# Pairs of 512-column subtractions joined into 1024-column ones, one more convolution job in seven products, and ScalarE's output work emitted later

## The chip, the cores and the metric

The kernel runs on one core of a Trainium2 chip. The metric is the device time of one execution in microseconds (us), the median of several runs. A profiled execution of the same program gives the trace.

The engines are called as in the profile: PE (TensorE matmuls), PEld (its weight loads, which overlap PE), DVE (VectorE), ACT (ScalarE), POOL (GpSimd) and SP (which only issues DMAs here).

## The reference

One layer of a hybrid decoder on x of 512 positions by 1024 channels, in float32:

```
h = rmsnorm(x, norm_mix_g)
proj = h @ w_in                       # 1024 x 9232
bg, cg, xv, q, k, v, z, a, b, ga, gb = split(proj)
y_a = (bg * causal_dwconv(cg * xv, conv_a_w)) @ w_a_out
y_b = gdn_branch(q, k, v, z, a, b, ...) @ w_b_out
mix = sigmoid(ga) * y_a + sigmoid(gb) * y_b
x = x + mix @ w_o
h = rmsnorm(x, norm_ffn_g)
up = causal_dwconv(h @ w_up, ffn_conv_w);  gate, val = split(up)
x = x + (silu(gate) * val) @ w_down
return rmsnorm(x, norm_final_g)
```

`gdn_branch` is a gated delta rule over 8 heads of 128, in chunks: a recurrence of small matmuls. bg, cg, xv, ga, gb, q, k, v and z have 1024 columns each; w_up has 5632.

## The kernel before

**Jobs.** The products with weights are cut into jobs of 256 output columns, and `run_jobs` (L225) runs them one after the other. The order is: 16 jobs for k, q, v and z of the delta rule; GB0 to GB3; then the convolution jobs CG0, XV0, BG0, CG1, XV1, BG1 and so on to BG3; GA0 to GA3; then w_a_out, w_b_out, w_o, w_up and w_down. While PE works on job i, the weights of job i+1 are prepared and those of job i+2 to i+4 are loaded, 1 MB a job in four quarters of 128x512.

**Precision.** Every operand is split into a rounded high part and the rest: ACT casts a 128x512 quarter to the high part `wh` (L159), and DVE subtracts it from the quarter for the low part `wl` (L160). `mm3` (L117) then makes three matmuls for each product (high x low, low x high, high x high). `wh` and `wl` are pools of WQ = 12 tiles each; a new tile waits until PE has read the tile that was there.

**Plain jobs.** `col_job` (L261) makes 2 output banks x 8 row tiles x 3 = 48 matmuls of 512 columns, from four quarters.

**Seven-product jobs.** `sum_job` (L320) cuts the 1024x256 weight block and the activations into 2x2 quarters and makes seven products in place of eight (a Strassen form): 7 x 4 x 3 = 84 matmuls of 256 columns. For this `SumBlock.split` (L174) prepares seven forms, called 11, 12, 22, s3, s2, s4 and s1, of which the last four are sums of quarters: four DVE operations on the raw block (L182), seven casts and seven subtractions. PE uses the forms in the order 11, 12, s3, s2, s4, 22, s1 in three banks A, B, C. Four `snap` copies on ACT (L139) save a bank's half while PE goes on: u after 11, v after s3, u after s2, v after s4. Form s2 writes over what the first u copy reads, 22 over what the first v copy reads, s1 over what the second u copy reads; so PE waits for these copies.

**Outputs.** After 22 `firsts` (L346) is queued, after s1 `seconds` (L350): each is one DVE addition (L347, L351) that makes half of the job's output, and `seconds` goes on with the job's consumer: a sigmoid on ACT for GB and GA; for XV a multiplication by CG's output (L1262) and a convolution of one ACT operation (L391) and two DVE taps (L394) for each half; for BG two multiplications (L1271); nothing for CG.

**What sets the order.** PE, ACT and DVE each run their queue strictly in the program's order. The kernel's Python writes the order: after each 2048 columns of matmuls `tick` (L96) takes a step of each of several queues of generators: one of the delta rule's three (backs, mids, chains), two of `evacs` (the outputs), one of `splits` (the next block's preparation), one of `sums_of`. A `yield` ends a step. A scheduler then orders the instructions that are ready, and `tc.issue_after` (L135) keeps the s casts and the consumers behind the last snap.

Of the 28 jobs that could go in seven products, 27 do: GB1 to GB3, all convolution jobs but XV1 (L1279), GA0 to GA2, and ten of w_up. XV1 is plain.

Of the kernel before, what the change touches and what calls it, by code (L numbers as in the profile page):

```python
# [9 lines left out]
F32 = mybir.dt.float32  # L10
F32R = mybir.dt.float32r
AF = mybir.ActivationFunctionType
ALU = mybir.AluOpType
# [3 lines left out]
P = 128  # L17
S = 512
# [8 lines left out]
C_BG, C_CG, C_XV, C_Q, C_K, C_V, C_Z, C_GA, C_GB = range(0, 36, 4)  # L27
# [4 lines left out]
WQ = 12  # L32
# [29 lines left out]
def layer_kernel(ctx, tc, x, norm_mix_g, w_in, w_ab, conv_a_w, gdn_conv_w, gdn_A_log, gdn_dt_bias,  # L62
# [3 lines left out]
    pe, act, dve, pool = nc.tensor, nc.scalar, nc.vector, nc.gpsimd  # L66
# [6 lines left out]
    wp = ctx.enter_context(tc.tile_pool(name="wp", bufs=2))  # L73
# [3 lines left out]
    def nm(s):  # L77
        cnt[0] += 1
        return f"{s}{cnt[0]}"

    def bank():
        return ps.tile([P, 512], F32, tag="ps", name=nm("ps"))
# [50 lines left out]
    snaps = []  # L133

    def after(ins):  # L135
        return tc.issue_after(ins) if ins else nullcontext()

    def snap(out, in_):
        snaps.append(act.copy(out=out, in_=in_).ins)  # L139

    class Block:
        def __init__(self, src, quarter=(4, P)):
            self.src, self.quarter = src, quarter
            self.raw, self.ready, self.lead, self.fed, self.fine = None, False, 2, True, False
            self.wh, self.wl, self.behind = {}, {}, None
# [6 lines left out]
            for lo, hi in [(q, q + 1) for q in range(4)] if self.fine else [(0, 4)]:  # L152
                nc.sync.dma_start(out=self.raw[:, lo:hi], in_=src[:, lo:hi])

        def part(self, name, src):
            wh = wp.tile([P, S], F32R, tag="wh", bufs=WQ, name=nm("wh"))
            wl = wp.tile([P, S], F32R, tag="wl", bufs=WQ, name=nm("wl"))
            with after(snaps[-1] if name in ("s1", "s2", "s3", "s4") and snaps else self.behind):
                act.copy(out=wh, in_=src)  # L159
            dve.tensor_tensor(out=wl, in0=src, in1=wh.bitcast(F32), op=ALU.subtract)  # L160
            self.wh[name], self.wl[name] = (t if len(self.quarter) == 1 else t.rearrange("p (k n) -> p k n", n=P)
                                            for t in (wh, wl))

        def split(self):
            if self.ready:
                return
            self.ready = True
            for q in range(4):
                self.part(q, self.raw[:, q])
                yield  # L170


# [1 line left out]
    class SumBlock(Block):  # L174
        def split(self):
            if self.ready:
                return
            self.ready = True
            r = [self.raw[:, q] for q in range(4)]

            def to(q, a, b, op):
                dve.tensor_tensor(out=r[q], in0=a, in1=b, op=op)  # L182

            self.part("11", r[0])
            yield
            self.part("12", r[1])
            yield
            self.part("22", r[2])
            yield
            to(2, r[3], r[2], ALU.add)  # L190
            to(3, r[0], r[3], ALU.subtract)
            self.part("s3", r[3])
            yield
            to(0, r[2], r[0], ALU.subtract)
            self.part("s2", r[0])
            yield
            to(1, r[1], r[0], ALU.subtract)
            self.part("s4", r[1])
            yield
            self.part("s1", r[2])  # L200
            yield


    class FormBlock(Block):
# [12 lines left out]
        def split(self):  # L217
            if self.ready:
                return
            self.ready = True  # L220
            for q, name in enumerate(self.names):
                self.part(name, self.raw[:, q])
                yield

    def run_jobs(jobs):  # L225
# [35 lines left out]
    def col_job(w, i, xs, consume, pre=None):  # L261
        def use(wh, wl):
            if pre:
                pre()
            x_ = xs() if callable(xs) else xs
            for j in range(GW // P):
                o = bank()
                products(o, wh, wl, j, x_)
                evacs.append(Task(consume(j, o)))
        return Block(lambda: w[i]), use  # L270
# [49 lines left out]
    def sum_job(w, i, xs, sums, consume, place, pre=None, uv=None, near=lambda: None):  # L320
        def use(wh, wl):
            if pre:
                pre()
            drain(sums_of)
            x_, ts, low = xs() if callable(xs) else xs, sums(), near()
            A, B, C = bank(), bank(), bank()
            L, R = slice(0, HS), slice(HS, S)
            dst = place()
            u, v = uv() if uv else (scratch("u"), scratch("v"))

            def times(o, form, b, first):
                mm3(o, [(wh[form][:, k], wl[form][:, k], b[0][:, k], b[1][:, k]) for k in range(ND // 2)],
                    first, not first)

            def quarter(K, T):
                if K and low:
                    return [low[e][T] for e in range(2)]
                return [x_[e][:, K * 4:K * 4 + 4, T * HS:T * HS + HS] for e in range(2)]

            def t(i_):  # L340
                return [ts[e][i_] for e in range(2)]

            d = dst.rearrange("p (j t c) -> p t j c", j=2, t=2)
            pair = lambda a: a.rearrange("p (j c) -> p j c", j=2)

            def firsts():  # L346
                dve.tensor_tensor(out=d[:, 0], in0=pair(B), in1=pair(u), op=ALU.add)  # L347
                yield

            def seconds():  # L350
                dve.tensor_tensor(out=d[:, 1], in0=A[:, L].unsqueeze(1).broadcast_to([P, 2, HS]), in1=pair(v),  # L351
                                  op=ALU.add)
                yield
                yield
                for j in range(2):
                    rest = consume(j, dst[:, j * S:(j + 1) * S])
                    while True:
                        with after(snaps[-1]):
                            got = next(rest, rest)
                        if got is rest:  # L360
                            break
                        yield

            times(A[:, L], "11", quarter(0, 0), True)
            snap(u[:, L], A[:, L])
            times(B[:, L], "12", quarter(1, 0), True)
            times(B[:, R], "s3", t(2), False)
            snap(v[:, R], B[:, R])
            times(A[:, L], "s2", t(1), False)
            snap(u[:, R], A[:, L])  # L370
            times(C[:, L], "s4", quarter(1, 1), True)
            snap(v[:, L], C[:, L])
            times(B[:, R], "22", t(3), False)
            evacs.append(Task(firsts()))
            times(A[:, L], "s1", t(0), False)
            evacs.append(Task(seconds()))
        return SumBlock(lambda: w[i]), use

# [39 lines left out]
    hT = [hp.tile([P, ND, S], F32R, tag=f"h{i}", name=f"hT{i}") for i in range(2)]  # L418
# [100 lines left out]
    with tc.tile_pool(name="st1", bufs=1) as st1:  # L519
# [80 lines left out]
        def out_lo(lo, bs, k):  # L600
            dve.scalar_tensor_tensor(out=hT[1][:, k, lo:lo + HS], in0=bs[k // 2][:, (k % 2) * HS:(k % 2 + 1) * HS],  # L601
                                     scalar=wA[:, 120 + k:121 + k], in1=hT[0][:, k, lo:lo + HS].bitcast(F32),
                                     op0=ALU.mult, op1=ALU.subtract)

        def round_k(q):
            wh = wp.tile([P, S], F32R, tag="wh", bufs=WQ, name=nm("wh"))
            act.copy(out=wh, in_=k_block.raw[:, q])
            k_block.wh[q] = wh.rearrange("p (k n) -> p k n", n=P)

        def rest_k(q):  # L610
            wl = wp.tile([P, S], F32R, tag="wl", bufs=WQ, name=nm("wl"))
            dve.tensor_tensor(out=wl, in0=k_block.raw[:, q], in1=k_block.wh[q].rearrange("p k n -> p (k n)").bitcast(F32),
                              op=ALU.subtract)
            k_block.wl[q] = wl.rearrange("p (k n) -> p k n", n=P)
# [552 lines left out]
    hsums = lambda: st["ts"]  # L1167
# [90 lines left out]
    def xv_c(g):  # L1258
        def c(j, o):
            m = 2 * g + j  # L1260
            u = held[g][:, j * S:(j + 1) * S]
            dve.tensor_tensor(out=u, in0=o, in1=u, op=ALU.mult)  # L1262
            c_ = tmp("c", 2)
            yield from conv(c_, u, ca_w(m), 3)
            held["c", m] = c_
        return c
# [8 lines left out]
    near = lambda: st.get("near")  # L1275
    for g in range(4):
        jobs += [sum_job(w_in, C_CG + g, hT, hsums, nothing, cg_place(g), None if g else open_conv,
                         near=near if g else lambda: None),
                 sum_job(w_in, C_XV + g, hT, hsums, xv_c(g), pair_out, near=near) if g != 1 else  # L1279
                 col_job(w_in, C_XV + g, hT, xv_c(g)),  # L1280
                 sum_job(w_in, C_BG + g, hT, hsums, bg_c(g), pair_out, near=near)]

    def ga_c(g):
# [343 lines left out]
    def xs():  # L1627
        if "xs" not in st:
            st["xs"] = [place(st["up"], f"t{e}", f"xs{e}") for e in range(2)]
        return st["xs"]  # L1630
# [208 lines left out]
```

## Time and profile before

| what | before |
|---|---|
| median of 3 runs | 945.96 us (945.27 to 946.88) |
| the profiled execution | 946.38 us |
| its span | 944.6 us |
| PE busy | 932.1 us (99%) |
| PEld busy | 823.0 us (87%) |
| DVE busy | 777.0 us (82%) |
| ACT busy | 546.4 us (58%) |
| granted PE clock | 1.00 nearly throughout |

The span runs from the first to the last instruction; 1.8 us of the execution lie outside it. A timeline row has the start in us, the duration, the engine, the line, the operation, out<-in, the shapes and a count; in square brackets stands the idle time of the engine before it and what ended it. A row with a count is several instructions in a run. A matmul's duration is longer than its distance to the next one, since they are pipelined, so PE's pace is read from starts. DVE's and ACT's instructions overlap at their ends too.

### The profile page before, as it was taken

The page shows a single profiled execution, that of the slowest core. Times are in us where ns is not written, and L with a number is a line of the kernel's source. Part 1 is how long each engine was busy: PE and PEld are TensorE (multiplying, and loading weights), DVE is VectorE, ACT ScalarE, POOL GpSimd, SP SyncE. Part 2 cuts the span into 40 slices and gives each one's busy share as a digit, 9 for nine tenths or more (in the row PEclk, how much of TensorE's full clock was granted, in tenths as well). Part 3 has the DMA queues.
Part 4 walks back from the last instruction along what each step waited for, and adds up shares of the span by engine and source line. Part 5 has one row for each costly group of instructions (what it writes and reads, how often), then busy time and mean ns, then how long its engine had stood idle before and what let it go on. Part 6 is the DMA issues. An engine that isn't in the chain of part 4 may idle for free.

```text
span 944.6 us, 17664 instructions
## 1 busy us (share of the span) xinstructions
PE 932.1 (99%) x6512; PEld 823.0 (87%) x6512; DVE 777.0 (82%) x1448; ACT 546.4 (58%) x1202; POOL 177.5 (19%) x288
## 2 busy tenths in 40 slices
PE   8999999999999999999999999999999999999996
PEld 6888887887889999999988888998899998888885
DVE  5978686898967989999753579998899898988885
ACT  6796756666465554555741246455565566556563
POOL 3330401304111121312342000322322210000001
PEclk9999999999999999999999999999999999999998
DMA  6443422213014568776797336586966675187332
GB/s 232 158 141 99 121 55 91 76 48 105 9 47 135 154 199 170 174 196 182 246 256 175 111 131 217 154 215 178 226 156 221 153 187 139 48 286 245 106 100 89
DMA packets 82902, 142.41 MB, mean 151 GB/s; under 512 B 24795, under 2 KB 29824, under 8 KB 80256
## 3 DMA queue, kind: packets, MB, share of 16 engines
q1 hardware_dynamic: 65904, 107.47, 34.7%
q0 software_dynamic: 16768, 33.56, 17.9%
q8 instruction: 51, 0.84, 0.3%
q14 instruction: 35, 0.29, 0.1%
q10 hardware_dynamic: 144, 0.26, 0.1%
HBM read 133.64 MB, written 32.78 MB: 176 GB/s over the span
## 4 chain that ended last, share of the span: by engine, by line
PE 85%; DVE 6%; ACT 3%; issue 2%; DMA 2%; POOL 1%; SPq 0%; POOLq 0%; DVEq 0%; ACTq 0%
PE ps L109 78%; DVE raw L182 2%; DVE wl L160 2%; PE ps L819 1%; PE ps L784 1%; DMA xt<-in_x_dram 1%; ACT wh L159 1%; PE ps L1022 1%; PE ps L1042 1%; DVE c L394 1%; PE ps L1031 1%; DMA raw<-in_w_in_dram 0%; PE ps L1010 0%; PE ps L1009 0%; PE ps L1480 0%
## 5 line engine op out<-in xcount | busy, mean ns | idle before, releaser
L159 ACT CAST wh<-raw 128x512 fp32r<-128x512 f32 x377 | 218.4, 621 | 129.2 <-PE ps L109 77.5
L160 DVE TENSOR_TENSOR wl<-raw,wh 128x512 fp32r<-128x512 f32 x377 | 251.0, 688 | 40.8 <-ACT wh L159 38.8
L109 PE MATMUL ps<-hT,wh 128*128 128x512 f32 (+1 forms) x888 | 251.6, 360 | 0.3 <-DVE hT L601 0.3
L109 PEld LDWEIGHTS ps<-hT,wh 128*128 128x128 f32 x888 | 156.9, 189 | 20.7 <-DVE hT L601 0.5
L109 PE MATMUL ps<-hT,wl 128*128 128x512 f32 (+1 forms) x444 | 152.1, 353 | 0.0
L109 PE MATMUL ps<-h,wh 128*128 128x512 f32 (+1 forms) x592 | 150.2, 341 | 0.0
L109 PEld LDWEIGHTS ps<-h,wh 128*128 128x128 f32 x592 | 103.2, 189 | 12.5
L109 PE MATMUL ps<-ts,wh 128*128 128x256 f32 x544 | 100.7, 279 | 1.6 <-ACT u L139 1.6
L109 PE MATMUL ps<-wh,xs 128*128 128x512 f32 (+1 forms) x320 | 96.5, 384 | 0.0
L109 PE MATMUL ps<-h,wl 128*128 128x512 f32 (+1 forms) x296 | 96.0, 340 | 0.0
L109 PEld LDWEIGHTS ps<-hT,wl 128*128 128x128 f32 x444 | 83.8, 189 | 9.8
L109 PEld LDWEIGHTS ps<-ts,wh 128*128 128x128 f32 x544 | 84.9, 188 | 2.3 <-ACT u L139 2.2
L182 DVE TENSOR_TENSOR raw<-raw 128x512 f32<-128x512 f32 x108 | 74.3, 688 | 2.6
L109 PEld LDWEIGHTS ps<-wh,xs 128*128 128x128 f32 x320 | 59.6, 188 | 11.8
L109 PE MATMUL ps<-ts,wl 128*128 128x256 f32 x272 | 65.5, 277 | 0.0
L249 POOL COPY gate<-raw 1x1 f32<-1x1 f32 x38 | 22.1, 581 | 215.7 <-DMA raw<-in_w_up_dram 77.6
L109 PEld LDWEIGHTS ps<-h,wl 128*128 128x128 f32 x296 | 56.0, 189 | 6.3
L109 PE MATMUL ps<-wl,xs 128*128 128x512 f32 (+1 forms) x160 | 61.4, 384 | 0.0
L109 PE MATMUL ps<-us,wh 128*128 128x256 f32 x320 | 57.9, 277 | 0.0
L394 DVE SCALAR_TENSOR_TENSOR ct<-ps,wA,ct 128x511 f32<-128x511 f32 (+2 forms) x72 | 53.2, 741 | 3.9 <-ACT ct L391 3.7
L159 ACT CAST wh<-raws 128x512 fp32r<-128x512 f32 x66 | 39.7, 620 | 25.6 <-DVE wl L160 8.1
L160 DVE TENSOR_TENSOR wl<-raws,wh 128x512 fp32r<-128x512 f32 x66 | 43.3, 687 | 11.5 <-ACT wh L159 11.5
(341 smaller groups left out, 1792.2 us busy)
## 6 DMA issues: line engine op xcount, KB each, us to landing
raw<-in_w_up_dram SPq DMA_DIRECT2D x88, 256.0 KB, 4.6
raw<-in_w_in_dram SPq DMA_DIRECT2D x20, 1024.0 KB, 5.2
raw<-in_w_in_dram SPq DMA_DIRECT2D x64, 256.0 KB, 4.4
dv<-in_w_down_dram POOLq DMA_DIRECT2D x50, 256.0 KB, 6.8
raws<-in_w_down_dram SPq DMA_DIRECT2D x32, 256.0 KB, 4.4
raws<-dv SPq DMA_DIRECT2D x24, 256.0 KB, 5.3
ov<-in_w_o_dram POOLq DMA_DIRECT2D x20, 256.0 KB, 6.3
raw<-in_w_a_out_dram SPq DMA_DIRECT2D x16, 256.0 KB, 5.0
```

What stands on the lines that cost most here:

```text
L109: pe.matmul(o, lhsT=a, rhs=b, start=start, stop=stop, skip_group_check=free)
L159: act.copy(out=wh, in_=src)
L160: dve.tensor_tensor(out=wl, in0=src, in1=wh.bitcast(F32), op=ALU.subtract)
L182: dve.tensor_tensor(out=r[q], in0=a, in1=b, op=op)
L249: tc.keep_in_program_order(pool.tensor_copy(out=gate[:, 0:1], in_=el[:, 0:1]))
L394: dve.scalar_tensor_tensor(out=dst[:, sh:], in0=src[:, :S - sh], scalar=wcol(j), in1=dst[:, sh:], op0=ALU.mult, op1=ALU.add)
L784: pe.transpose(out=o[:, n * P:(n + 1) * P], in_=src[:, n * P:(n + 1) * P], identity=ident)
L819: pe.matmul(o[:, i], lhsT=kqs[:, a, h, 0, sl], rhs=kqs[:, b, h, :, sl], start=a > 0, stop=a + b == 0)
L1022: pe.matmul(o[:, 0:P], lhsT=TTf[:, f, :], rhs=rs[h], start=True, stop=True)
L1031: pe.matmul(o2[:, 0:P], lhsT=kn[:, f, :], rhs=vns[h], start=True, stop=True)
L1042: pe.matmul(o[:, 0:P], lhsT=A[:, f, :], rhs=vns[h], start=True, stop=True)
```

## The change

1. The two pools of 12 tiles become two tiles of 12 slots each (`ringh`, `ringl`), given out in turn. `parts` casts one or two quarters and makes one subtraction over both where their slots are neighbours: 1024 columns; a pair that falls on slots 11 and 0 is still two of 512.
2. In `SumBlock.split` the forms go in pairs: (11, 12), then 22 alone, (s3, s2), (s4, s1). The four sums are the same four numbers, made in another order: s3 is now the first sum made, where it was the second.
3. In `seconds` the consumer begins four yields, not two, behind the addition.
4. XV1 becomes a `sum_job`.

```diff
+    ring = [wp.tile([P, WQ, S], F32R, bufs=1, name=n) for n in ("ringh", "ringl")]
...
-        def part(self, name, src):
-            wh = wp.tile([P, S], F32R, tag="wh", bufs=WQ, name=nm("wh"))
-            wl = wp.tile([P, S], F32R, tag="wl", bufs=WQ, name=nm("wl"))
-            with after(snaps[-1] if name in ("s1", "s2", "s3", "s4") and snaps else self.behind):
-                act.copy(out=wh, in_=src)
-            dve.tensor_tensor(out=wl, in0=src, in1=wh.bitcast(F32), op=ALU.subtract)
...
+        def parts(self, names, qs):
+            at = ring_slots(len(names))
+            for name, q, a in zip(names, qs, at):
+                with after(snaps[-1] if name in ("s1", "s2", "s3", "s4") and snaps else self.behind):
+                    act.copy(out=ring[0][:, a], in_=self.raw[:, q])
...
+            cut = next((i for i in range(1, len(at)) if at[i] < at[i - 1]), len(at))
+            for lo, hi in ((0, cut), (cut, len(at))):
+                if lo < hi:
+                    wh, wl = (t[:, at[lo]:at[hi - 1] + 1] for t in ring)
+                    step = qs[1] - qs[0] if len(qs) > 1 else 1
+                    dve.tensor_tensor(out=wl, in0=self.raw[:, qs[lo]:qs[hi - 1] + 1:step], in1=wh.bitcast(F32),
+                                      op=ALU.subtract)
...
-            self.part("11", r[0])
-            yield
-            self.part("12", r[1])
-            yield
-            self.part("22", r[2])
-            yield
-            to(2, r[3], r[2], ALU.add)
-            to(3, r[0], r[3], ALU.subtract)
-            self.part("s3", r[3])
-            yield
-            to(0, r[2], r[0], ALU.subtract)
-            self.part("s2", r[0])
-            yield
-            to(1, r[1], r[0], ALU.subtract)
-            self.part("s4", r[1])
-            yield
-            self.part("s1", r[2])
+            self.parts(("11", "12"), (0, 1))
+            yield
+            yield
+            self.parts(("22",), (2,))
+            yield
+            to(0, r[0], r[3], ALU.subtract)
+            to(3, r[3], r[2], ALU.add)
+            yield
+            to(2, r[2], r[0], ALU.subtract)
+            self.parts(("s3", "s2"), (0, 2))
+            yield
+            to(1, r[1], r[2], ALU.subtract)
+            yield
+            self.parts(("s4", "s1"), (1, 3))
             yield
...
-                yield
-                yield
+                for _ in range(4):
+                    yield
...
-                 sum_job(w_in, C_XV + g, hT, hsums, xv_c(g), pair_out, near=near) if g != 1 else
-                 col_job(w_in, C_XV + g, hT, xv_c(g)),
+                 sum_job(w_in, C_XV + g, hT, hsums, xv_c(g), pair_out, near=near),
```

What it moves in the engines' queues is shown at three places. The line numbers of the changed kernel are higher by up to 14: L160 becomes L175, L182 L196, L347 L358, L351 L362, L159 L167, L1061 L1075, L1285 L1298.

ACT's queue at the start of job GA1, before. `mixa` is the output of the job in front, GA0, and L1285 its sigmoid, which waits for GA0's `seconds`; u and v are GA1's snaps; the casts belong to the next block.

```order
L159 CAST wh_5927<-raw_67 128x512 [waits DMAHW5_49,Activation_49]
L159 CAST wh_5941<-raw_67 128x512 [waits DMAHW6_49,Activation_49]
L159 CAST wh_5954<-raw_67 128x512 [waits DMAHW7_49,Activation_49]
L1285 ACTIVATE mixa_5778<-mixa_5778 128x512 [waits DMASW1_49,DMASW0_49,DVE_49]
L1285 ACTIVATE mixa_5778<-mixa_5778 128x512
L139 COPY u_5920<-ps_5917 128x256 [waits PE_49]
L159 CAST wh_5968<-raw_67 128x512 [waits DMAHW4_49,DVE_49]
L139 COPY v_5921<-ps_5918 128x256 [waits PE_49]
```

The same place after.

```order
L167 CAST ringh<-raw_67 128x512 [waits DMAHW6_49,Activation_49]
L167 CAST ringh<-raw_67 128x512 [waits DMAHW5_49,Activation_49]
L167 CAST ringh<-raw_67 128x512 [waits DMAHW4_49,PE_49]
L139 COPY u_5563<-ps_5560 128x256 [waits PE_49]
L1298 ACTIVATE mixa_5438<-mixa_5438 128x512 [waits DMASW1_49,DMASW0_49,DVE_49]
L1298 ACTIVATE mixa_5438<-mixa_5438 128x512
L139 COPY v_5564<-ps_5561 128x256 [waits PE_49]
L167 CAST ringh<-raw_67 128x512 [waits DVE_49,Activation_49]
```

The two sigmoids stood ahead of the first u copy and now stand behind it.

DVE's queue in job GB3, where the delta rule's last two heads end, before. L1052 feeds a power on POOL, for whose result `fac` the first L1061 waits; L347 and L351 are GB2's output, L160 the next block's preparation.

```order
L1052 SCALAR_TENSOR_TENSOR fac_3979<-sso_3714,ssq_2900 128x8 [waits Activation_49]
L1061 TENSOR_SCALAR AV_2683<-AV_2683,fac_3979 128x128 [waits Pool_49]
L347 TENSOR_TENSOR sgb<-ps_3774,ct_107 128x2x256 [waits PE_49]
L1061 TENSOR_SCALAR AV_2683<-AV_2683,fac_3979 128x128
L1061 TENSOR_SCALAR AV_2683<-AV_2683,fac_3979 128x128 [waits DVE_49] x2
L160 TENSOR_TENSOR wl_4028<-raw_67,wh_4027 128x512 [waits Activation_49]
L351 TENSOR_TENSOR sgb<-ps_3773,ct_107 128x2x256 [waits PE_49]
```

The same place after.

```order
L1066 SCALAR_TENSOR_TENSOR fac_3795<-sso_3547,ssq_2782 128x8 [waits Activation_49]
L358 TENSOR_TENSOR sgb<-ps_3607,ct_109 128x2x256 [waits PE_49]
L175 TENSOR_TENSOR ringl<-raw_67,ringh 128x1024 [waits Activation_49]
L362 TENSOR_TENSOR sgb<-ps_3606,ct_109 128x2x256 [waits PE_49]
L1075 TENSOR_SCALAR AV_2567<-AV_2567,fac_3795 128x128 [waits Pool_49]
```

The output additions and a joined subtraction now stand between the power's input and the wait for its result.

DVE's queue through job XV3, before, from CG3's `firsts` to the preparation of the next block's s forms.

```order
L347 TENSOR_TENSOR o_5361<-ps_5359,u_5362 128x2x256 [waits PE_49]
L160 TENSOR_TENSOR wl_5512<-raw_66,wh_5511 128x512 [waits DMAHW1_49,Activation_49]
L351 TENSOR_TENSOR o_5361<-ps_5358,v_5363 128x2x256 [waits PE_49]
L160 TENSOR_TENSOR wl_5525<-raw_66,wh_5524 128x512 [waits DMAHW2_49,Activation_49]
L160 TENSOR_TENSOR wl_5537<-raw_66,wh_5536 128x512 [waits DMAHW3_49,Activation_49]
L182 TENSOR_TENSOR raw_66<-raw_66 128x512 [waits DMAHW0_49,DVE_49]
L182 TENSOR_TENSOR raw_66<-raw_66 128x512 [waits DVE_49] x2
L160 TENSOR_TENSOR wl_5551<-raw_66,wh_5550 128x512 [waits Activation_49]
L182 TENSOR_TENSOR raw_66<-raw_66 128x512 [waits DVE_49,Pool_49]
L160 TENSOR_TENSOR wl_5565<-raw_66,wh_5564 128x512 [waits Activation_49]
L160 TENSOR_TENSOR wl_5578<-raw_66,wh_5577 128x512 [waits PE_49,Activation_49]
L160 TENSOR_TENSOR wl_5591<-raw_66,wh_5590 128x512 [waits PE_49,Activation_49]
```

The same job after.

```order
L358 TENSOR_TENSOR o_5072<-ps_5070,u_5073 128x2x256 [waits PE_49]
L362 TENSOR_TENSOR o_5072<-ps_5069,v_5074 128x2x256 [waits PE_49,Activation_49]
L175 TENSOR_TENSOR ringl<-raw_66,ringh 128x1024 [waits DMAHW2_49,DMAHW0_49,Activation_49]
L175 TENSOR_TENSOR ringl<-raw_66,ringh 128x512 [waits DMAHW1_49]
L196 TENSOR_TENSOR raw_66<-raw_66 128x512 [waits DMAHW3_49,DVE_49]
L196 TENSOR_TENSOR raw_66<-raw_66 128x512 [waits DVE_49] x2
L196 TENSOR_TENSOR raw_66<-raw_66 128x512 [waits DVE_49,Pool_49]
L175 TENSOR_TENSOR ringl<-raw_66,ringh 128x1024 [waits Activation_49]
L175 TENSOR_TENSOR ringl<-raw_66,ringh 128x1024 [waits DVE_49,PE_49,Activation_49]
```

Seven subtractions have become four, `firsts` and `seconds` stand side by side, and the four sums come in one run. Over the whole program 76 subtractions of 1024 columns stand in the changed queue; 8 of the 84 pairs fall on slots 11 and 0.

More of the change, by code (lines that the diff above doesn't have):

```diff
@@ L139, in snap, with ring_slots @@
         snaps.append(act.copy(out=out, in_=in_).ins)
+    ring = [wp.tile([P, WQ, S], F32R, bufs=1, name=n) for n in ("ringh", "ringl")]
+    nring = [0]
+    def ring_slots(n):
+        at = nring[0]
+        nring[0] = (at + n) % WQ
+        return [(at + i) % WQ for i in range(n)]
     class Block:
@@ L153, in load @@
                 nc.sync.dma_start(out=self.raw[:, lo:hi], in_=src[:, lo:hi])
-        def part(self, name, src):
-            wh = wp.tile([P, S], F32R, tag="wh", bufs=WQ, name=nm("wh"))
-            wl = wp.tile([P, S], F32R, tag="wl", bufs=WQ, name=nm("wl"))
-            with after(snaps[-1] if name in ("s1", "s2", "s3", "s4") and snaps else self.behind):
[L159 to L162, printed above, removed]
+        def parts(self, names, qs):
[3 more added lines that the diff above has]
+                    act.copy(out=ring[0][:, a], in_=self.raw[:, q])
+                self.wh[name], self.wl[name] = (t[:, a] if len(self.quarter) == 1 else
+                                                t[:, a].rearrange("p (k n) -> p k n", n=P) for t in ring)
+            cut = next((i for i in range(1, len(at)) if at[i] < at[i - 1]), len(at))
[5 more added lines that the diff above has]
+                                      op=ALU.subtract)
         def split(self):
@@ L168, in split @@
             for q in range(4):
-                self.part(q, self.raw[:, q])
+                self.parts((q,), (q,))
                 yield
@@ L221, in split @@
             for q, name in enumerate(self.names):
-                self.part(name, self.raw[:, q])
+                self.parts((name,), (q,))
                 yield
@@ L603, in out_lo @@
                                      op0=ALU.mult, op1=ALU.subtract)
+        at_k = {}
         def round_k(q):
-            wh = wp.tile([P, S], F32R, tag="wh", bufs=WQ, name=nm("wh"))
+            at_k[q], = ring_slots(1)
+            wh = ring[0][:, at_k[q]]
             act.copy(out=wh, in_=k_block.raw[:, q])
@@ L610, in rest_k @@
         def rest_k(q):
-            wl = wp.tile([P, S], F32R, tag="wl", bufs=WQ, name=nm("wl"))
+            wl = ring[1][:, at_k[q]]
             dve.tensor_tensor(out=wl, in0=k_block.raw[:, q], in1=k_block.wh[q].rearrange("p k n -> p (k n)").bitcast(F32),
```

## The prediction

> **What bounds the kernel now.** I read the page first: busy shares, and the chain of waits by engine.
>
> ```profile
> span 944.6 us, 17664 instructions
> PE 932.1 (99%) x6512; PEld 823.0 (87%) x6512; DVE 777.0 (82%) x1448; ACT 546.4 (58%) x1202; POOL 177.5 (19%) x288
> PE 85%; DVE 6%; ACT 3%; issue 2%; DMA 2%; POOL 1%; SPq 0%; POOLq 0%; DVEq 0%; ACTq 0%
> ```
>
> PE is busy nearly always, and the chain that ended last is PE's for 85%. The chain in order of time says where it is not.
>
> ```profile
> 319.10 71.65 PE ps L109 x576
> ...
> 446.80 145.47 PE ps L109 x705
> ...
> 612.19 316.09 PE ps L109 x1857
> ```
>
> From 446.8 us to 928.3 PE runs without a stop that matters: DVE time saved there, in w_up's ten seven-product jobs, buys nothing. Between 391 and 446.8 the chain runs through DVE and ACT. What PE waits for is one row of the waits, and where it waits the timeline of PE shows.
>
> ```profile
> PE ps L109 <- ACT u L139: 1.6, 3, 0.9
> ```
>
> ```profile
> 317.57 0.62 PE L109 MATMUL ps<-ts,wh 128*128 128x256 f32 x4
> 319.10 0.39 PE L109 MATMUL ps<-ts,wh 128*128 128x256 f32 x1 [0.91 <-ACT u L139]
> ...
> 439.64 0.62 PE L109 MATMUL ps<-ts,wh 128*128 128x256 f32 x4
> 440.45 0.38 PE L109 MATMUL ps<-ts,wh 128*128 128x256 f32 x1 [0.20 <-ACT u L139]
> ...
> 445.72 0.62 PE L109 MATMUL ps<-ts,wh 128*128 128x256 f32 x4
> 446.80 0.39 PE L109 MATMUL ps<-ts,wh 128*128 128x256 f32 x1 [0.46 <-ACT u L139]
> ```
>
> Three times a form waits for a u copy. ACT's timeline says why the copy was late.
>
> ```profile
> 317.63 1.15 ACT L1144 ACTIVATE sgb<-sgb 128x512 f32<-128x512 f32 x2 [3.15 <-DVE sgb L351]
> 318.69 0.35 ACT L139 COPY u<-ps 128x256 f32<-128x256 f32 x1
> ...
> 439.50 0.62 ACT L159 CAST wh<-raw 128x512 fp32r<-128x512 f32 x1 [2.94 <-DVE raw L182]
> 440.03 0.36 ACT L139 COPY u<-ps 128x256 f32<-128x256 f32 x1
> ...
> 445.33 1.15 ACT L1285 ACTIVATE mixa<-mixa 128x512 f32<-128x512 f32 x2 [1.08 <-DVE mixa L351]
> 446.39 0.35 ACT L139 COPY u<-ps 128x256 f32<-128x256 f32 x1
> ```
>
> Twice two sigmoids stand ahead of the copy and wait for `seconds` on DVE; once a cast that waits for a raw sum. Behind all three is a late DVE.
>
> **The change part by part.** PE's pace and DVE's load come from the windows (span, then busy and count of PE, PEld, DVE).
>
> ```profile
> 353.59:364.47 10.88, 10.88 (x50) 9.01 (x49) 10.63 (x18) 4.56 (x8) 1.64 (x3) 1.00 0.95 188
> 383.69:393.29 9.60, 9.60 (x86) 9.60 (x85) 8.54 (x14) 5.36 (x11) 2.14 (x4) 1.00 0.79 244
> 392.31:422.43 30.12, 30.12 (x266) 30.12 (x265) 29.51 (x49) 16.67 (x36) 7.83 (x12) 1.00 0.73 180
> ```
>
> *XV1 in seven products.* The first window is XV1 as a plain job, 10.88 us; the second XV2, a seven-product job of 84 matmuls, 9.60 (0.114 each). On PE's path the edit takes off 1.28 us.
>
> *Stalls.* The stall at 319.10: four matmuls from 317.57 end their turns at 318.03, so 1.07 us, and 0.11 more since the next one follows after 0.22: 1.18. In the same way 0.46 at 440.45 and 0.73 at 446.80, 2.37 together. DVE's timeline holds the rest of the ledger.
>
> ```profile
> 351.99 0.69 DVE L160 TENSOR_TENSOR wl<-raw,wh 128x512 fp32r<-128x512 f32 x1 [2.44 <-ACT wh L159]
> ...
> 392.31 0.68 DVE L347 TENSOR_TENSOR o<-ps,u 128x512 f32<-128x512 f32 x1
> 392.91 1.28 DVE L160 TENSOR_TENSOR wl<-raw,wh 128x512 fp32r<-128x512 f32 x2
> ...
> 422.43 0.69 DVE L347 TENSOR_TENSOR o<-ps,u 128x512 f32<-128x512 f32 x1
> ...
> 432.53 0.68 DVE L347 TENSOR_TENSOR o<-ps,u 128x512 f32<-128x512 f32 x1
> ...
> 438.06 2.15 DVE L182 TENSOR_TENSOR raw<-raw 128x512 f32<-128x512 f32 x3
> ...
> 543.33 1.23 DVE L1365 TENSOR_TENSOR mix<-o,mix 128x1024 fp32r<-128x1024 f32 x1 [0.39 <-ACT mix L1357]
> 544.47 1.22 DVE L1365 TENSOR_TENSOR mix<-mixa,mix 128x1024 fp32r<-128x1024 f32 x1
> ```
>
> *What a joined subtraction saves.* By durations one would say 2 x 0.69 - 1.22 = 0.16 us. But the pair at 392.91 lasts 1.28, so the second starts 0.60 behind the first, and the two of 1024 columns start 1.14 apart: the ends overlap. A pair costs 1.20 in the queue and 1.14 joined: 0.06 saved, 0.18 a block. The Trainium skill (VectorE: DVE Perf Modes, "The DRAIN you can't avoid") says that the next operation doesn't start until the pipe has emptied, and advises fewer operations; by that a block would save about 0.47. The starts 0.60 apart with durations of 0.69 speak against it, so it gets only a rival's chance.
>
> *DVE's debt.* From XV2's `firsts` (392.31) to XV3's (422.43) DVE needs 30.12 us for three blocks and the consumers, while PE needs 3 x 9.60 = 28.80: DVE falls back 1.32 a group, from 0.98 before the next job's start (393.29) to 0.34 behind it (422.09). Before, the plain XV1 repaid this: DVE idled 2.44 us at 351.99. After, a group costs 30.12 - 3 x 0.18 = 29.58 and falls back 0.78, but XV1's block brings 3 x 1.14 + 0.60 of subtractions, four sums (three at 0.73, from the 2.15 for three, and 0.60) and 1.20 of output additions, 8.01, where a plain block needs 4 x 0.60 = 2.40. Nothing is repaid: from -0.98 at XV0, the earliest that PE's 22 allows, three groups give +1.36 at XV3, 1.02 later than now. DVE's saving is thus spent on PE's saving.
>
> *What that does to the stalls.* Of the three, the two behind sigmoids go: ACT's order now has the first u copy ahead of them, and the v copy behind them isn't needed until form 22, two forms or 24 matmuls (2.7 us) later. The one behind the cast stays: the cast for s3 now needs one raw sum, not two, and so comes 0.73 sooner for the same DVE, but DVE is 1.02 later: 0.46 + 1.02 - 0.73 = 0.75. For the jobs ahead of it with the same order (CG3 above all) I add 0.3, an estimate from half of what GA0 shows. So 1.18 + 0.73 + 0.46 - 0.75 - 0.3 = 1.3 comes off.
>
> *GB2 and GB3.* The delta rule ends here, and DVE's 1024-column pieces stand between its small operations.
>
> ```profile
> 293.91 0.61 DVE L1024 TENSOR_SCALAR vn<-ps,ap 128x128 f32<-128x128 f32 x2 [0.21 <-PE ps L1022]
> ...
> 303.98 0.29 DVE L1061 TENSOR_SCALAR AV<-AV,fac 128x128 f32<-128x128 f32 x1 [2.14 <-POOL fac L1053]
> ```
>
> ```profile
> 294.89 0.61 PE L1031 MATMUL ps<-vn,KU 128*128 128x128 f32 x4
> ```
>
> PE's L1031 takes vn 0.37 after its last one ended (294.52). A 1.14 us piece that starts just ahead of vn delays it by up to 1.1, so PE by 0 to 0.7; over the few steps I take +0.3, and -0.3 to +1.0 as bounds. On the other side DVE's 2.14 us idle for POOL is now covered by an addition, a pair and an addition; that makes DVE early for CG0, which I have counted with the stall at 319.10.
>
> *At nothing:* the ring of slots (the same 12; each write waits for the same readers), the sums' new order, and the two extra yields on w_up's outputs, since PE doesn't wait there; if the outputs came late enough to hold a bank, each would cost what a stall above costs, under 1.2.
>
> *Sum:* -1.28 - 1.3 + 0.3 = -2.3 us. On the profiled execution's 946.38 (span 944.6 and 1.8 outside) that is 944.1; on the median of 945.96, 943.6 with rounding. A difference under 0.2%, 1.9 us, is no change that a measurement of this kernel can tell.
>
> **The rivals.** *DVE keeps up (0.19).* If the joined pieces save more than 0.06, as the skill's rule has it, or the new order removes small waits, a group needs under 28.80; 0.47 a block gives 30.12 - 1.41 = 28.71. All stalls go: -1.28 - 2.37 = -3.65, 942.3. For it: 30.12 holds some 0.6 of gaps. Against: the 0.60.
>
> *The debt eats the gain (0.23).* If pairs lose on waits what they save, a group stays at 30.12, DVE enters GA0 at -0.98 + 3 x 1.32 = 2.98, 2.64 later than now, and that stall is 0.46 + 2.64 - 0.73 = 2.4; with the 0.3 above: -1.28 - 1.18 - 0.73 + 1.9 + 0.3 = -1.0, 945.0.
>
> *A pair waits for its second cast (0.05, slower).* (s4, s1) can't begin until ACT has cast both; where DVE has nothing else, that is one cast, 0.62, a block. A group is then 31.44, and DVE falls back 2.64; four groups' worth to GA1 are 10.6, of which about 3 is slack (0.98 and some 2 that the new order bears): 7.5 of stalls, -1.28 - 2.37 + 7.5 = +3.9, 949.8. It turns slower than now from 1.66 a group, a wait of 0.29 a block. Against: the four sums stand together, and a sum (0.60) covers most of a cast.
>
> *A seven-product job isn't cheaper (0.02).* Then only the stalls count, and weights bind: the second window has PEld busy 9.60 of 9.60, the plain one 9.01 of 10.88. If XV1 cost 10.88 still: -1.3 + 0.3 = -1.0, 945.0. The Trainium skill (TensorE: Matmul & The Clock Gate, "Back-to-back issue gap") gives 81 ns a matmul at 128 columns and 131 at 512, so some 98 at 256, an estimate: 8.2 us against 6.3, a loss of 1.9. The windows, 9.60 against 10.88, disagree and decide.
>
> **How the numbers follow.** The forecast has 0.51; its own range, with the bounds of GB's term and a CG stall of 0 to 0.6, is 942.9 to 944.7. Below 944.1 lies about 0.38 of the 0.51, and with the first rival's 0.19 faster has 0.57. The rest of the forecast, 0.13, the debt's 0.23 and 0.02 make 0.38 within 0.2%. Slower has 0.05. The range from 942.2 (the first rival) to 945.8 (beyond the debt by GB's upper bound) leaves out the last rival and tails.
>
> **What would show it.** Right: XV1 in 9.60 us; no wait for a u copy behind sigmoids; joined subtractions 1.14 apart; XV3's `firsts` about 1.4 us behind its job's end; one stall of about 0.7 near GA0, and PE without a stop behind it. Wrong: PE waits for vn or S in GB2 and GB3 over 1 us; waits for ACT ahead of joined subtractions; PE waiting for `wl` itself; new idle time of PE in w_up.

## The result and the profile after

The changed kernel takes 953.42 us, median of 5 runs (951.23 to 956.49), against 946.17 (945.27 to 946.88) before: a ratio of 1.0077, 95% interval 1.0055 to 1.0100. It is slower by 7 us where the forecast was faster by 2.3. Its profiled execution took 953.42, with a span of 951.7; the span before was 944.6, so 7.1 us have to be found.

The page: busy times, and the chain of waits by engine.

```profile
span 951.7 us, 17614 instructions
PE 932.1 (98%) x6548; PEld 825.1 (87%) x6548; DVE 775.5 (81%) x1379; ACT 547.2 (57%) x1209; POOL 178.5 (19%) x288
PE 78%; DVE 11%; ACT 4%; issue 3%; DMA 3%; POOL 1%; POOLq 0%; SPq 0%; DVEq 0%; ACTq 0%
```

PE's busy time is the same 932.1 although XV1 got shorter, and DVE has 1379 instructions where it had 1448. By these sums the 7 us are idle time; that XV1's 1.28 us don't show in PE's busy time has its reason further down, where PE goes on at half pace. The timeline of PE in GA2, the third gate job, shows nearly all of the loss in one place.

```profile
459.06 0.62 PE L109 MATMUL ps<-ts,ringh 128*128 128x256 f32 x4
465.40 0.58 PE L109 MATMUL ps<-ts,ringh 128*128 128x256 f32 x1 [5.73 <-ACT u L139]
465.78 0.42 PE L109 MATMUL ps<-ts,ringl 128*128 128x256 f32 x1
466.00 0.41 PE L109 MATMUL ps<-ts,ringh 128*128 128x256 f32 x1
```

A matmul's turn is the time from its start to the next one's, 0.114 us here. Four matmuls from 459.06 end their turns at 459.52, and the next one starts at 465.40: 5.9 us. Behind that they start 0.21 to 0.22 apart where 0.114 was the pace. The windows of PE say why (the column before the last two is the granted clock).

```profile
455.00:459.00 4.00, 4.00 (x37) 4.00 (x36) 0.28 (x1) 0.64 (x2) 0.08 (x1) 1.00 0.96 268
465.40:467.00 1.60, 1.60 (x7) 1.60 (x8) 0.00 (x0) 1.60 (x4) 0.00 (x0) 0.50 1.05 189
468.00:469.00 1.00, 1.00 (x5) 0.81 (x5) 1.00 (x2) 1.00 (x3) 0.00 (x0) 0.50 0.80 311
470.00:471.00 1.00, 1.00 (x6) 0.84 (x5) 1.00 (x3) 1.00 (x3) 0.00 (x0) 1.00 0.70 221
```

From 465.4 to 469 PE has half its clock: 12 matmuls of 256 columns and two of 512 take twice their turns, 12 x 0.1 + 2 x 0.2 and some tenths, 1.7 us. The Trainium skill (TensorE: Matmul & The Clock Gate, "What's actually happening") has the clock go to half after at least one idle window of about 3.4 us and come back after at least one as long busy one; 5.9 us idle and some 3.7 at 0.50 behind them agree with that.

PE waits for a u copy on ACT again. ACT's timeline in this job, first before, then after.

```profile
457.68 1.14 ACT L387 CAST yas<-ya 128x512 fp32r<-128x512 f32 x2 [0.42 <-PE ps L109]
458.73 0.36 ACT L139 COPY u<-ps 128x256 f32<-128x256 f32 x1
458.99 1.14 ACT L387 CAST yas<-ya 128x512 fp32r<-128x512 f32 x2
460.03 0.37 ACT L139 COPY v<-ps 128x256 f32<-128x256 f32 x1
460.30 2.19 ACT L159 CAST wh<-raw 128x512 fp32r<-128x512 f32 x4
```

```profile
455.55 0.37 ACT L139 COPY v<-ps 128x256 f32<-128x256 f32 x1 [0.28 <-PE ps L109]
463.43 0.62 ACT L167 CAST ringh<-raw 128x512 fp32r<-128x512 f32 x1 [7.50 <-DMA raw<-in_w_a_out_dram]
463.95 1.14 ACT L398 CAST yas<-ya 128x512 fp32r<-128x512 f32 x2
464.99 0.36 ACT L139 COPY u<-ps 128x256 f32<-128x256 f32 x1
```

Before, no weight cast stood between the last three copies of this job; those of w_a_out came behind the last v copy. After, one cast stands alone ahead of the u copy and waits 7.50 us for a transfer of w_a_out, with the copy queued behind it. The chain of waits says which transfer.

```profile
453.99 0.71 DVE ringl L175 x2
454.71 8.64 DMA raw<-in_w_a_out_dram
463.43 0.26 ACT ringh L167
463.95 1.14 ACT yas L398 x2
465.08 0.28 ACT u L139
465.40 9.70 PE ps L109 x40
```

It is a quarter issued at 454.71, the last but one of the eight that SP issues from 450.31 to 456.02: the third of the second block of w_a_out (WA1), which PE needs two jobs later. Its cast was put ahead of the casts of WA0, which come at 466.56. Nothing in the source asks for that. In the kernel before, `wh` and `wl` were tiles of a pool; in the changed one they are slots of two tiles that the kernel hands out itself, and here the scheduler no longer places the casts in the order in which they are written. Why it doesn't, no run shows; that the ring is what lets it, e2 below does.

The third loss is at the transposes after w_o (timeline of PE).

```profile
598.25 0.39 PE L109 MATMUL ps<-ringh,mix 128*128 128x512 f32 x1
599.42 0.63 PE L1493 MATMUL ps<-ident,hn 128*128 128x128 f32 x4 [0.78 <-DVE hn L1484]
```

The ledger: PE came to GA2 1.33 us earlier than before (451.11 against 452.44), then lost 5.9 + 1.7, then 0.9 at 598, where it had lost 0.1 before (0.35 from 591.87 to 592.22, with a turn of 0.23); -1.3 + 7.6 + 0.8 = 7.1, the difference of the spans.

### The profile page after: what moved, and what is told of

Read it like the earlier page. It is cut to its first block, busy times and chain, and to the rows that moved or that the text cites. A ratio compares the mean times of both kernels' runs of the same rounds, so it can differ in the third digit from the quotient of the medians.

```text
span 951.7 us, 17614 instructions
## 1 busy us (share of the span) xinstructions
PE 932.1 (98%) x6548; PEld 825.1 (87%) x6548; DVE 775.5 (81%) x1379; ACT 547.2 (57%) x1209; POOL 178.5 (19%) x288
## 4 chain that ended last, share of the span: by engine, by line
PE 78%; DVE 11%; ACT 4%; issue 3%; DMA 3%; POOL 1%; POOLq 0%; SPq 0%; DVEq 0%; ACTq 0%
PE ps L109 70%; DVE ringl L175 3%; DVE raw L196 3%; DMA raw<-in_w_in_dram 2%; PE ps L798 1%; PE ps L833 1%; ACT ringh L167 1%; DVE c L405 1%; DMA raw<-in_w_a_out_dram 1%; DVE o L362 1%; PE ps L1036 1%; PE ps L1056 1%; DVE o L358 1%; PE ps L577 1%; DVE ya L1285 1%
## 5 line engine op out<-in xcount | busy, mean ns | idle before, releaser
L167 ACT CAST ringh<-raw 128x512 fp32r<-128x512 f32 x380 | 222.0, 620 | 141.7 <-PE ps L109 82.9
L175 DVE TENSOR_TENSOR ringl<-raw,ringh 128x512 fp32r<-128x512 f32 (+1 forms) x302 | 244.6, 826 | 50.1 <-ACT ringh L167 48.9
L109 PE MATMUL ps<-hT,ringh 128*128 128x512 f32 (+1 forms) x864 | 243.8, 359 | 0.6 <-ACT hT L608 0.4
L109 PEld LDWEIGHTS ps<-hT,ringh 128*128 128x128 f32 x864 | 152.6, 189 | 19.9 <-ACT hT L608 0.6
L109 PE MATMUL ps<-h,ringh 128*128 128x512 f32 (+1 forms) x592 | 150.3, 341 | 0.0
L109 PE MATMUL ps<-hT,ringl 128*128 128x512 f32 (+1 forms) x432 | 147.2, 352 | 0.0
L109 PE MATMUL ps<-ts,ringh 128*128 128x256 f32 x576 | 107.8, 281 | 7.1 <-ACT u L139 5.9
L109 PEld LDWEIGHTS ps<-h,ringh 128*128 128x128 f32 x592 | 103.2, 189 | 12.7 <-DVE h L1498 0.2
L109 PE MATMUL ps<-ringh,xs 128*128 128x512 f32 (+1 forms) x320 | 96.7, 384 | 0.0
L109 PE MATMUL ps<-h,ringl 128*128 128x512 f32 (+1 forms) x296 | 96.0, 340 | 0.0
L196 DVE TENSOR_TENSOR raw<-raw 128x512 f32<-128x512 f32 x112 | 77.0, 688 | 2.6
L167 ACT CAST ringh<-raws 128x512 fp32r<-128x512 f32 x66 | 39.5, 620 | 25.9 <-PE ps L109 8.5
```

The source lines that it names most:

```text
L109: pe.matmul(o, lhsT=a, rhs=b, start=start, stop=stop, skip_group_check=free)
L167: act.copy(out=ring[0][:, a], in_=self.raw[:, q])
L175: dve.tensor_tensor(out=wl, in0=self.raw[:, qs[lo]:qs[hi - 1] + 1:step], in1=wh.bitcast(F32), op=ALU.subtract)
```

## The experiments

Theory H: the cast that ran ahead, let through by the ring of slots, is the loss. Theory D, its rival: late transfers and a late DVE are the cause, and PE must wait for them somewhere. Beside the first four kernels the kernel before took 945.69 us (21 runs); beside the later ones its time is given with them.

**e1, the changed kernel with the cast held back.** One line of run_jobs: every block's casts are queued behind the last copy, and not only if the job just emitted made one. PE's order is the same as in the changed kernel. On ACT the cast of WA1 goes back behind the v copy; some casts and loads in w_up's last jobs move too, where PE waits in neither kernel.

```
-            if i + 2 < len(jobs) and len(snaps) > n:
+            if i + 2 < len(jobs) and snaps:
                 jobs[i + 2][0].behind = snaps[-1]
```

> The changed kernel, with the casts of every block (the second block of w_a_out among them) held behind the last u or v copy; ACT's queue then has no cast of w_a_out ahead of GA2's u copy. Theory H (the cast that the ring of slots let run ahead waits 7.5 us for its transfer, and GA2's u copy waits behind it): the 5.9 us stall of PE and the 1.7 us at half pace behind it go, so 953.4 - 7.6 = 945.8 us. Theory D (transfers land late because DVE and the raw blocks run late, and PE must wait for them somewhere): the wait comes back at GA3 or in w_a_out, and the time stays at 950 us or more.

Measured: 945.25 us (11 runs, 944.18 to 947.66), ratio 1.0002, interval 0.9993 to 1.0010. The stall and the half clock are gone and come back nowhere near GA3: theory H holds, D falls. But the gain that was forecast doesn't come either: 945.25 is level with the kernel before. The profiled execution came to GA3 1.8 us earlier than before (460.42 against 462.20) and lost it at the transposes (timelines of PE and of ACT).

```profile
590.09 0.39 PE L109 MATMUL ps<-ringh,mix 128*128 128x512 f32 x1
592.59 0.63 PE L1493 MATMUL ps<-ident,hn 128*128 128x128 f32 x4 [2.11 <-DVE hn L1484]
```

```profile
579.16 2.19 ACT L167 CAST ringh<-raw 128x512 fp32r<-128x512 f32 x4 [2.34 <-DMA raw<-in_w_o_dram]
```

A second cast had run ahead: the first of these four waits for the quarter of w_o that was issued last (574.12), while the other three find theirs landed. DVE waits for it (1.98 us, up to 580.34) ahead of the additions that lead to `hn`.

**e2, the kernel before with the ring alone.** No joined subtraction, no new order of sums, two yields, XV1 plain. Shown is the edit in `part`; the block of k gets its slots in the same way.

```
-            wh = wp.tile([P, S], F32R, tag="wh", bufs=WQ, name=nm("wh"))
-            wl = wp.tile([P, S], F32R, tag="wl", bufs=WQ, name=nm("wl"))
+            at, = ring_slots(1)
+            wh, wl = (t[:, at] for t in ring)
```

> The kernel before with the ring of slots in place of the pool's tiles, and nothing else: no joined subtraction, two yields, XV1 plain. Theory H: the same cast now stands ahead of GA2's u copy, and PE stalls there until the transfer has landed; with 5 to 8.6 us from the issue at about 454.5 to the landing, the stall is 2 to 6 us and with the half pace behind it the time 948 to 954 us. Theory D (the ring itself costs nothing, late DVE does it): 945.9 to 946.4 us, as before.

Measured: 951.63 us (5 runs, 950.01 to 954.43), ratio 1.0067, interval 1.0054 to 1.0081. The same cast, the same wait (ACT's timeline, then PE's):

```profile
463.06 0.62 ACT L167 CAST ringh<-raw 128x512 fp32r<-128x512 f32 x1 [6.89 <-DMA raw<-in_w_a_out_dram]
463.58 1.13 ACT L395 CAST yas<-ya 128x512 fp32r<-128x512 f32 x2
464.62 0.36 ACT L139 COPY u<-ps 128x256 f32<-128x256 f32 x1
```

```profile
459.30 0.62 PE L109 MATMUL ps<-ts,ringh 128*128 128x256 f32 x4
465.04 0.58 PE L109 MATMUL ps<-ts,ringh 128*128 128x256 f32 x1 [5.12 <-ACT u L139]
```

So the ring alone, put into the kernel before, costs 5.9 us by the medians (the trace is of the slowest of the five runs, 954.43, with a pause of 5.3 and 2.9 more at half clock), and the changed kernel without the cast that it let ahead is no slower than before. The cause is shown from both sides.

**e3, the kernel before with XV1 in seven products alone.**

```
-                 sum_job(...) if g != 1 else
-                 col_job(w_in, C_XV + g, hT, xv_c(g)),
+                 sum_job(w_in, C_XV + g, hT, hsums, xv_c(g), pair_out, near=near),
```

> The kernel before with XV1 in seven products, and nothing else. By the ledger of DVE in the prediction: -1.28 for the job, and DVE, which isn't repaid, falls back 1.32 a group, so that the stall at GA0 grows by about 2.6: 946.2 - 1.3 + 2.6 = 947.5 us. If DVE keeps up (its idle 2.44 us beside the plain job was slack, no repayment): 944.9 us.

Measured: 948.84 us (5 runs, 948.46 to 950.25), ratio 1.0039, interval 1.0027 to 1.0052. Alone, the edit loses 3.2 us. Its trace has five waits for u copies, at 318, 380, 410, 440 and 456 us, of 0.9, 0.6, 1.0, 0.9 and 0.7 (counted as the prediction counts, with the 0.11 of the slower restart), and PE makes two more short stops of 0.2 (389 and 419): together 4.5 where the kernel before has 2.37. From GB2 to GA3 the kernel thus takes 175.4 us (287.16 to 462.55) against 174.3 (287.93 to 462.20): 1.1 more, though XV1 is 1.28 shorter. That fits the debt of DVE, for which 1.3 was forecast. The rest lies behind GA3, where the order moved as well: three waits of PE in w_up, of 1.8, 0.6 and 0.3. The largest is one for a copy of `h` that POOL's DMA makes (PE's timeline):

```profile
673.08 0.62 PE L109 MATMUL ps<-us,wh 128*128 128x256 f32 x4
675.46 0.38 PE L109 MATMUL ps<-hk,wh 128*128 128x256 f32 x1 [1.77 <-DMA hk<-h]
```

**e4, the kernel before with four yields alone** (in `seconds`, `for _ in range(4): yield` for two yields).

> The kernel before with four yields in place of two ahead of an output's second half, and nothing else. By the prediction the two stalls behind sigmoids (1.18 at GB3's end, 0.73 at GA0's) go and nothing comes for them: 946.2 - 1.9 = 944.3 us. If outputs that come later are late for DVE's or ACT's next work: 946 us or more.

Measured: 945.05 us (11 runs, 944.58 to 945.37), ratio 0.9992, interval 0.9983 to 1.0001: 0.6 us, where the interval just reaches 1. The wait behind GA0's sigmoids (446.80 before) went; at GB3's end the two sigmoids still stand ahead of the u copy (316.64 and 317.70 in ACT's timeline) and PE still waits 0.9. So the yields alone don't take that wait away. The ring alone doesn't either (1.0 at 318.56 in e2). With the new order of sums it is gone, with two yields too (e8, e10), and without joining too (e6, e9). So the new order of sums is what is left to explain it, though no run has that alone.

**e5, the changed kernel with casts in written order.** Each weight cast is queued on ACT behind the one written before it. This tests the mechanism as such: the ring and its slots stay, and the order of the casts is fixed.

```
+                with after(...), after(casts[-1] if casts else None):
+                    casts.append(act.copy(out=ring[0][:, a], in_=self.raw[:, q]).ins)
```

> The changed kernel, with every weight cast queued on ACT behind the cast that the program writes before it (pairs, yields and XV1 as in the change). Theory O (what the ring of slots took away is the order of the casts: two casts ran ahead of their loads, WA1's third quarter in GA2 and, with that one held, one of w_o at 579 us): PE is 1.8 us ahead when it comes to GA3, the wait of 2.3 us for hn at 590 shrinks to under 0.6, and the time is 943.5 to 944.3 us. Rival (the stage at 590 us is set by DVE's own chain to hn, whatever the order of the casts): the wait takes the 1.8 us again, 945.3 us, as the kernel with the held casts. If casts in a fixed order block one another elsewhere: above 946 us.

Measured: 944.74 us (11 runs, 943.89 to 945.29; the kernel before 945.54 in 33 runs beside this one and the next three), ratio 0.9992, interval 0.9983 to 1.0000. It falls between the two numbers. The wait for `hn` shrank as theory O says, from 2.3 to 0.2 (PE's timeline):

```profile
589.10 0.39 PE L109 MATMUL ps<-ringh,mix 128*128 128x512 f32 x1
589.57 0.63 PE L1494 MATMUL ps<-ident,hn 128*128 128x128 f32 x4
```

so the stage at 590 isn't bound by DVE's own chain. And with the ring still in place the loss is gone: it was the order of the casts, not the waits of the slots. PE comes to GA3 at 459.44, 2.8 us earlier than before; part of that was gained ahead of GB2 (287.37 against 287.93). What is missing is lost behind GA3, most of it in w_up, the largest piece where PE waits for a v copy at 712:

```profile
711.13 0.62 PE L109 MATMUL ps<-hk,ringh 128*128 128x256 f32 x4
712.37 0.38 PE L109 MATMUL ps<-us,ringh 128*128 128x256 f32 x1 [0.63 <-ACT v L139]
```

**e6, e5 with the pairs not joined** (`parts` issues one subtraction a slot; the rest is e5).

> The changed kernel with casts in written order, and each pair of slots in two subtractions of 512 columns in place of one of 1024; sums, casts, yields and XV1 as in the change. By the prediction (a joined pair saves 0.06 us, 0.18 a block) DVE falls back 0.5 us a group more, and the stalls from XV2 to GA1 grow by 1 to 1.5 us together: e5 + 1.2. If a pair loses on its wait for the second cast, or by freeing its raw block later, what it saves: e5 or below.

Measured: 945.88 us (11 runs, 944.88 to 947.92), ratio 1.0006, interval 0.9997 to 1.0015: e5 + 1.1, as the prediction's 0.06 a pair has it, and where it said: from GB2 to GA3 173.2 us (285.60 to 458.75) against 172.1 in e5 (287.37 to 459.44). The timelines of DVE give the size of a group from XV2's `firsts` to XV3's, joined (e5) and not (e6):

```profile
391.14 0.68 DVE L359 TENSOR_TENSOR o<-ps,u 128x512 f32<-128x512 f32 x1
...
420.83 0.68 DVE L359 TENSOR_TENSOR o<-ps,u 128x512 f32<-128x512 f32 x1
```

```profile
389.53 0.69 DVE L358 TENSOR_TENSOR o<-ps,u 128x512 f32<-128x512 f32 x1
...
419.81 0.68 DVE L358 TENSOR_TENSOR o<-ps,u 128x512 f32<-128x512 f32 x1
```

29.69 against 30.28: 0.59 for three blocks, 0.54 was forecast.

**e7, e5 with XV1 plain again.**

> The changed kernel with casts in written order, and XV1 plain again. By the prediction XV1 costs 1.28 us more on PE, and the repaid DVE takes away what is left of the stalls behind late casts (0.8 + 0.3 + 0.2 in the run with held casts): within 0.5 us of e5. If DVE's debt is no cause of these stalls, they stay, and it is e5 + 1.3.

Measured: 943.62 us (11 runs, 942.98 to 944.25), ratio 0.9979, interval 0.9970 to 0.9988: faster than e5 by 1.1, which neither branch had. The matmuls on the sums of activations (first and last start) bracket the stages with GB, the convolutions and GA, in e5 and in e7:

```profile
L109 PE MATMUL ps<-ts,ringh x576: 276/276/388, 276.4 to 459.3; 128*128 128x256 f32 x192
```

```profile
L109 PE MATMUL ps<-ts,ringh x544: 276/276/388, 275.8 to 458.8; 128*128 128x256 f32 x182
```

182.9 and 183.0 us: in these stages XV1 in seven products buys nothing, as the ledger of DVE said (the first branch). The 1.1 lies behind them, from there to the end of the span 484.3 (943.6 - 459.3) against 483.1 (941.9 - 458.8): some 0.7 in w_up, of which 0.4 is the wait at 712 (it is shorter in e7), and 0.45 behind the last matmul, a piece that differs by as much among all these traces (7.3 to 8.0). XV1 in seven products uses seven slots in place of four, and the order behind it moves; which part of that costs the 0.7 was not separated.

**e8, e5 with two yields again.**

> The changed kernel with casts in written order, and two yields again in place of four. By the prediction the stalls behind sigmoids come back (1.18 at GB3's end, some 0.7 at GA0's): e5 + 1.9. By the run of the four yields alone, which gave 0.6 us and left 0.8 of the stall at GB3's end: e5 + 0.6.

Measured: 945.02 us (11 runs, 944.10 to 946.03), ratio 0.9994, interval 0.9985 to 1.0003: e5 + 0.3, less than either number, and less than the 11 runs of either kernel spread. The yields are worth some tenths at most here.

**e9 and e10: e7 without joining, and e7 with two yields** (the kernel before 945.65 in the 21 runs beside them).

> The changed kernel with casts in written order, XV1 plain, and each pair in two subtractions of 512 columns (the run with XV1 plain, without joining). If joining pays only by lowering DVE's debt in the convolution stage, it pays little here, where the plain XV1 repays: within 0.4 us of e7's 943.6. If it pays wherever blocks in seven products follow one another (GB, w_up too), the 1.1 us between e5 and e6 come again: 944.7 us.

> The changed kernel with casts in written order, XV1 plain and two yields (the run with XV1 plain, without the later outputs). e8 against e5 gave 0.3 us for the yields, e4 against the kernel before 0.6: e7 + 0.3 to 0.6, 943.9 to 944.2 us. If the yields are worth the whole 1.9 us of the stalls behind sigmoids here: 945.5 us.

Measured: 945.20 us (11 runs, 944.52 to 945.70 and one of 5311; ratio 0.9997, interval 0.9988 to 1.0006) and 944.32 us (11 runs, 943.56 to 945.42, ratio 0.9986, interval 0.9977 to 0.9995). Without joining e7 loses 1.6, more than either number. The traces say where: from GB2 to GA3 only 0.3 (172.4 us against 172.1), as the first branch has it, but 1.2 at two waits for v copies in w_up, at 711.50 and 772.87: 0.89 and 0.59 us of idle time, against 0.25 and none in e7. The kernel before, which joins nothing, waits at neither place, so what joining saves there hangs on the rest of the change. Without the later outputs e7 loses 0.7, and not behind sigmoids, where the wait is 0.2 (443.54): the largest piece is a wait of 1.1 for a u copy in w_up, at 790.67.

e7 is the best of these: joined subtractions, new order of sums, later outputs, casts in written order, XV1 plain; 1.9 us faster than the kernel before (ratio 0.9979) and, by the two ratios, some 9 faster than the changed one (1.0077 - 0.9979 of 945.5).

## Why the prediction was wrong, point by point

- **The step that failed** stands under "At nothing": "the ring of slots (the same 12; each write waits for the same readers)". The slots are as many, but the order in ACT's queue isn't the same, and the order is what costs: e5 keeps the slots, fixes the order and takes 944.74. A cast was placed ahead of the copies of GA2, ACT waited 7.5 us for its data, and PE paid 5.9 us and then 1.7 at half clock. The ring alone costs 5.9 us (e2), and with that one cast held the changed kernel is level with before (e1). Neither the sum nor any rival had this term, and ACT's order in GA2 was not among the places looked at; it would have shown the cast.
- **XV1 in seven products, -1.28**: right as a duration. The windows after have it at

```profile
352.48:362.08 9.60, 9.60 (x87) 9.60 (x85) 9.29 (x13) 5.82 (x13) 1.78 (x3) 1.00 0.69 167
393.66:422.90 29.24, 28.01 (x242) 27.62 (x241) 28.68 (x40) 16.17 (x35) 7.95 (x13) 1.00 0.74 180
```

  9.60. As a gain it is nothing: e7 against e5 shows it repaid in the stages that follow, which the prediction's debt said in its mechanism ("DVE's saving is thus spent on PE's saving") but not in its sum.
- **A joined pair, 0.06**: right. Two joined subtractions last 2.35 us together (DVE's timeline), so the second starts 1.13 behind the first.

```profile
441.01 2.35 DVE L175 TENSOR_TENSOR ringl<-raw,ringh 128x1024 fp32r<-128x1024 f32 x2
```

  The group from 393.66 to 422.90 takes 29.24, with 29.58 forecast, and e5 against e6 measures 0.59 for the 0.54. The rival by the Trainium skill (VectorE: DVE Perf Modes, "The DRAIN you can't avoid"), 0.47 a block, would have made 1.41 of it; the runs disagree. (The same section adds that a next operation that is not held starts earlier, and that is what the 1.13 shows at durations of 1.22.)
- **DVE's lag**: the number came, by luck. XV3's `firsts` start at 422.90, 1.38 behind the end of its job at 421.52, with 1.36 forecast. But a group earlier, where the same steps give 0.58 (-0.98 + 2 x 0.78), the lag was 2.78 (393.66 against 390.88): DVE had just idled 2.11 us for a cast on ACT, and that for a load that took 9.2 us (383.11 to 392.32). PE then waited 1.2 us for a v copy, which the prediction took to have 2.7 us to spare (timelines of DVE and PE).

```profile
393.05 0.69 DVE L175 TENSOR_TENSOR ringl<-raw,ringh 128x512 fp32r<-128x512 f32 x1 [2.11 <-ACT ringh L167]
```

```profile
398.96 0.38 PE L109 MATMUL ps<-ts,ringh 128*128 128x256 f32 x1 [1.04 <-ACT v L139]
```

  In e5, with the casts in order, DVE doesn't idle there, and the lags are 0.69 and 0.93, nearer to the ledger's 0.58 and 1.36 than the changed kernel is along the way.
- **The stalls, -1.3**: about half of it came, -0.7 in e1. From GB2 (288.01, and 287.93 before) to GA3 PE gains 1.86; less 1.28 for XV1, with the 0.14 of GB below put back. The wait at GB3's end went; one stays near GA0 (0.3, with 0.75 forecast), and the convolutions have two in the changed kernel (1.2 at 398 and 0.3 at 410, with 0.3 in all forecast; 0.8 and 0.35 in e1). The mechanism given for the first was wrong: the later sigmoids alone leave 0.9 of its 1.18 (e4), and by exclusion the new order of sums took it away, though no run has that alone.
- **GB2 and GB3, +0.3**: both kernels start GB2 at 287.93, and CG0 starts at 313.92 against 313.78: +0.14.
- Up to GA3 the sum thus holds in size: forecast -2.3, measured -1.9 in e1. **What came behind it failed a second time**: "From 446.8 us to 928.3 PE runs without a stop that matters". True of the trace before, but PE waited for `hn` there already, by 0.1 us, so any gain ahead of that point holds only if DVE's chain moves with it. In e1 a second early cast kept it from moving. The rest of that sentence, "DVE time saved there, in w_up's ten seven-product jobs, buys nothing", failed too for the changed order: there e9, without joining, waits 1.2 us longer in w_up than e7.
- **The rival on the slower side**, a pair that waits for its second cast, didn't happen: a group would have taken 31.44.

## What to carry to other kernels

When tiles of a pool are replaced by slots that the kernel hands out, the order of the instructions that fill them may change: compare, queue by queue, where each instruction that waits for a transfer now stands, and tie such instructions to the order of their loads. An instruction placed early costs nothing by itself and everything by what is queued behind it. Where a second engine sets the pace, shortening a job on the first one can be repaid within a few jobs: the joined operations on DVE gave 1.1 to 1.6 us here, measured in the changed kernel with ordered casts, and the shorter job on PE nothing.

## What the runs showed of the hardware

In the changed kernel the granted clock was 1.00 up to 462.2 us, 2.7 us into the pause of 5.9, and 0.50 from there to 469.1; in e2 it was 1.00 up to 464.3, 4.6 us into a pause of 5.3, and 0.50 to 471.1. Both times it stood at a half for 6.8 us. What of that lay behind the pause, 3.7 and 6.1 us, cost 1.7 and 2.9 us, so two pauses of nearly one length cost 7.6 and 8.2. The Trainium skill (TensorE: Matmul & The Clock Gate, "What's actually happening") states at least one idle and at least one busy window of about 3.4 us each, which run freely and need not begin with a pause; 6.8 us at a half agrees with that, while a drop 2.7 us into a pause is sooner than one whole idle window. Behind the pause of 2.3 us in e1 the clock stayed at 1.00.

The 256 KB quarter that the cast waited for took 8.64 us from its issue to its landing, 9.13 in e2, where the median of SP's loads from 440 to 475 us was 5.3. SP's eight loads and POOL's transfers of w_down were under way together, at a DMA share of 0.96 (455 to 459 us); that this made the load slow is likely, but no run tests it.
